# The first weights of a decoder-layer kernel in quarters, on two DMA queues

## The chip, the cores and the metric

The kernel runs on one core of one Trainium2 chip. The metric is the device time of one execution in microseconds. A time is given as the median of several runs; one execution was also taken by the hardware profiler, and all rows of the profile come from that one. TensorE (PE) multiplies matrices, VectorE (DVE) and ScalarE (ACT) work on tensors in SBUF, GpSimd (POOL) helps, and SyncE (SP) issues most DMAs. ScalarE can issue DMAs too, on a queue of its own (ACTq beside SPq).

## What is computed

One layer of a hybrid decoder on 256 tokens of width 2048, all in float32:

```python
h = rmsnorm(x, norm_mix_g)
u = h @ w_in                                  # ten column groups
ya = b_g * causal_dwconv3(c_g * xa, conv_w) * silu(za)
yb = rmsnorm_per_head(hgrn2_chunked(silu(q), kk, iv, log_f)) * hg_norm_g * silu(og)
m = sigmoid(ga) * (ya @ w_a_out) + sigmoid(gb) * (yb @ w_b_out)
x = x + m @ w_o
gate = sigmoid(rmsnorm(x, ple_norm_g) @ w_ple_gate)
x = x + gate * (p @ w_ple_proj)               # p: 256 tokens x 256 features
return rmsnorm(x, final_norm_g)
```

The part around the change is the first product of the program, `p @ w_ple_proj`: 256 features are two k tiles of 128, and the 2048 output columns are four groups of 512.

## The kernel before

A float32 operand is split into a high part in the float32r form and a low part, the rest (`cut` at L198 for weights: ScalarE copies the high part at L199, VectorE subtracts at L200; `put` at L318 for activations). A product is then three matmuls, high by high, high by low, low by high (L1157 to L1159). Activations are the stationary operand, 128 features by 128 tokens, and weights stream through, 512 columns at a time, into a PSUM bank for each of the two token tiles.

The whole program is one list, `items`, in an order written out by hand. An item is a chunk of two k tiles by 512 columns of one weight matrix, 512 KB. The first four items (`PP`) are w_ple_proj, one item for each group of 512 columns; item 4 (`FIRST`) begins the big projection w_in. The raw chunks of two items share a buffer (`raw`), are cut a few items ahead of their use into `whi` and `wlo`, and used by the loop at L1226.

At the start, eight matmuls on zeros keep TensorE busy (L1046). The first loads are issued by hand (L278 to L293): `load_half(pos, i, eng)` loads k tile i of item pos, 128 x 512 floats, 256 KB, on the queue of `eng`. ScalarE's queue carries the two halves of item 0; SyncE's carries p (`praw`, two k tiles of 128 x 256 floats, 128 KB each, L280), item 1, the parameters `prm_t` (36 KB, gains and small weights; L284), items 2 and 3, and then w_in and x. Each load takes the next of eight DMA counters in turn, so a load's issue waits for the landing of the load eight before it. ScalarE's own work in the same order stands behind its DMA issues: a table load (L303), then the cuts.

For items 0 to 2 the cuts go by halves, and for item 0 p's k tiles are put between them: `put_p(0)` (high part by VectorE, L323, low part at L326), first half of the weights, `put_p(1)` (high part by ScalarE, L325), second half. Item 0's matmuls have an order of their own, so that what is there first is used first:

```python
for a, b in ((0, hi), (1, hi), (0, lo)):
    for t in range(NT):
        nc.tensor.matmul(psum[t], state[opname][a][:, k, t * P : (t + 1) * P], b[:, s], ...)
```

Here `a` is the part of p (0 high, 1 low), `b` that of the weights, `t` the token tile, and `s` the 512 columns of k tile k. These are six matmuls for each k tile.

Of the kernel before, what the change touches and what calls it, by code (L numbers as in the profile page):

```python
# [15 lines left out]
P = 128  # L16
T = 256
NT = T // P
# [5 lines left out]
CW = 512  # L24
# [24 lines left out]
def hybrid_kernel(ctx, tc, xT, x, pT, prm, gfin, masks, w_in, w_a, w_b, w_o, w_pg, w_pp, out):  # L49
    nc = tc.nc  # L50
# [23 lines left out]
    state = {"tmp": "tmp1"}  # L74
# [3 lines left out]
    def nm(s):  # L78
        uid[0] += 1
        return f"{s}_{uid[0]}"  # L80
# [5 lines left out]
    def bank(tag):  # L86
        return ps.tile([P, CW], F32, tag=tag, bufs=4, name=nm(tag))
# [19 lines left out]
    items = []  # L107
# [21 lines left out]
    def raw_of(pos):  # L129
        it = items[pos]  # L130
        if it["raw"] not in loaded:
            if it["kind"] == "S" and it["op"] == "hT":
                t = tuple(
                    pools["st"].tile([P, n, CW], F32, tag=tag, bufs=bufs, name=nm(tag))
                    for tag, n, bufs in (("sA", 2, 2), ("sB", 1, 3))
                )
            else:
                n = it["c"] if it["j"] == 0 else 4 + 4 * (it["j"] - 1) + it["c"] // 2
                spare = it["op"] == "x1T" and n in (5, 10, 14)
                pool, bufs = (pools["late"], 1) if spare else (wp, 3)  # L140
                t = pool.tile([P, 2, 2 * CW], F32, tag="raw", bufs=bufs, name=nm("raw"))
            loaded[it["raw"]] = t
        return loaded[it["raw"]]

    def load(pos):
        it = items[pos]
        if it["raw"] not in loaded:
            raw, (w, g, c) = raw_of(pos), it["w"]
            if it["kind"] == "S" and it["op"] == "hT":
                for n, to in enumerate(raw):  # L150
                    nc.sync.dma_start(out=to.rearrange("p n x -> p (n x)"), in_=w[g + n, :, c, n * CW :])
            elif it["kind"] in ("S", "C"):
                for n in range(2):
                    nc.sync.dma_start(out=raw[:, n, :], in_=w[g + n, :, c, :])
            elif pos < APART:
                for i in range(2):
                    w, g, c = items[pos + i]["w"]
                    nc.sync.dma_start(out=raw[:, i, :], in_=w[g, :, c, :])
            else:
                nc.sync.dma_start(out=raw, in_=w[g, :, c : c + 2, :])  # L160
# [27 lines left out]
    def free_pair(until):  # L188
        if "back" not in state:
            held.append([until, pair_of(wp, 4)])  # L190
            del held[:-4]
            return held[-1][1]
        it = min(held, key=lambda it: it[0])
        assert it[0] < state["pos"]
        it[0] = until if until < last_group else len(items)
        return it[1]

    def cut(hi, lo, src):  # L198
        a = nc.scalar.activation(out=hi, in_=src, func=AF.Copy)  # L199
        v = nc.vector.tensor_tensor(out=lo, in0=src, in1=hi.bitcast(F32), op=ALU.subtract)  # L200
        state["splits"] = (a.ins, v.ins)

    def split(pos, halves=(0, 1)):
        it = items[pos]
        load(pos)
        src = raw_of(pos)
        if it["kind"] == "S" and it["op"] == "hT":
            src = src[0].rearrange("p n x -> p (n x)")
        else:
            src = src[:, it["slot"], :]  # L210
        if pos not in parts:
            parts[pos] = free_pair(pos)
        hi, lo = parts[pos]
        s = slice(halves[0] * CW, (halves[-1] + 1) * CW)
        cut(hi[:, s], lo[:, s], src[:, s])

    def combine_late(pos):
# [43 lines left out]
    prm_t = const.tile([P, PRM_N], F32, name="prm_t")  # L261
    praw = pools["tmp1"].tile([P, 1024], F32, tag="X", bufs=4, name="praw")[:, : 2 * T]
# [10 lines left out]
    def load_half(pos, i, eng):  # L273
        w, g, c = items[pos]["w"]
        s = slice(i * CW, (i + 1) * CW)
        eng.dma_start(out=raw_of(pos)[:, pos % 2, s], in_=w[g, :, c, s])

    load_half(0, 0, nc.scalar)  # L278
    for k in range(2):
        nc.sync.dma_start(out=praw[:, k * T : (k + 1) * T], in_=pT[:, k, :])  # L280
    load_half(0, 1, nc.scalar)
    for i in range(2):
        load_half(1, i, nc.sync)
    nc.sync.dma_start(out=prm_t, in_=prm)  # L284
    for c in (2, 3):
        for i in range(2):
            load_half(c, i, nc.sync)
# [473 lines left out]
    def ep_products(op, bk):  # L761
        for n in ("ga", "gb"):
            state[n] = t4(n, 1) if op == "hT" else t4()
        a0, a1, b0, b1 = quarters()
        nc.scalar.activation(out=a0, in_=bk["P1"], func=AF.Copy)
        add(b1, a0, bk["P6"])
        nc.vector.tensor_tensor(out=b0, in0=bk["P5"], in1=b1, op=ALU.subtract)
        add(a1, b1, bk["P7"])
        nc.vector.tensor_tensor(out=b1, in0=bk["P5"], in1=a1, op=ALU.subtract)

    def ep_gates(op, n, bk):
        q = quarters()
        for t in range(NT):
            add(q[2 * n + t], q[2 * n + t], bk["c", n, t])
        if op != "hT":
            active.append(ep_pg(n, q[2 * n : 2 * n + 2]))
            return
        for t in range(NT):
            d = q[2 * n + t]
            nc.scalar.activation(out=d, in_=d, func=AF.Sigmoid, scale=state["rstd1"][:, t : t + 1])  # L780
# [380 lines left out]
    def product(psum, op, k, t, hi, lo, first, last):  # L1161
        triple(psum, tuple(x[:, k, t * P : (t + 1) * P] for x in op), (hi, lo), first, last)
# [3 lines left out]
    def count_products(gi):  # L1166
        order = [it for it in items if it["kind"] in ("S", "C") and it["gi"] == gi]
        used.clear()
        left.clear()
        for it in order:  # L1170
            for name in names_of(it):
                left[name] = left.get(name, 0) + 1
# [53 lines left out]
    for pos, it in enumerate(items[:last_group]):  # L1226
        mark, state["pos"] = len(nc.cur_bb.bb.instructions), pos
        kind, j, c, last = (it[n] for n in ("kind", "j", "c", "last"))
        _, _, w, g, opname = groups[it["gi"]]
        nch = w.shape[2]  # L1230
# [48 lines left out]
        if pos == NORM + 4:  # L1279
# [3 lines left out]
            for i in range(4):  # L1283
                z = slice(i * Q, (i + 1) * Q)
                nc.sync.dma_start(out=near_m[z], in_=masks[z, :NARROW, z])
                nc.sync.dma_start(out=full_m[z, :, z], in_=masks[z, NARROW:, z])
        if kind in ("S", "C"):
            if c == 0 and it.get("n", 0) == 0:
                count_products(it["gi"])
                c00, c01, c10, c11 = (("c", i, t) for i in range(2) for t in range(NT))  # L1290
                order = ("P6", c01, "P5", "P7", "P1", c00, c10, c11)
                if it["op"] != "hT":
                    order = ("P1", "P6", "P5", "P7", c00, c01, c10, c11)
                for name, tag in zip(order, "ggggssss"):
                    banks[name] = bank(tag)
            if pos == settled + 2 or it["op"] == "hT" and kind == "C" and c == nch - 1 and it["n"] == 0:
                ep_products(it["op"], banks)
            unit_products(pos)
            if kind == "C" and c == nch - 1:
                ep_gates(it["op"], it["n"], banks)  # L1300
        else:
            if c == 0:
                psums[it["gi"]] = [bank("s" if kind == "PP" and j >= 2 else "g") for _ in range(NT)]
            psum = psums[it["gi"]]
            hi, lo = parts.pop(pos)
            for i in range(2):
                k = 2 * c + i
                s = slice(i * CW, (i + 1) * CW)
                if pos == 0:
                    for a, b in ((0, hi), (1, hi), (0, lo)):  # L1310
                        for t in range(NT):
                            nc.tensor.matmul(  # L1312
                                psum[t], state[opname][a][:, k, t * P : (t + 1) * P], b[:, s],
                                start=k == 0 and a == 0 and b is hi, stop=k == 2 * nch - 1 and b is lo,
                            )
                    continue
                for t in range(NT):
                    product(psum[t], state[opname], k, t, hi[:, s], lo[:, s], k == 0, k == 2 * nch - 1)
# [39 lines left out]
    for t, halves in ((0, (0, 1)), (1, (0,)), (1, (1,))):  # L1358
        bk, n = bank("g"), CW // 2
        for c in range(nlast):  # L1360
# [3 lines left out]
            hi, lo = parts[last_group + c]  # L1364
            for i in range(2):
                k = 2 * c + i
                s = slice(i * CW + halves[0] * n, i * CW + (halves[-1] + 1) * n)
# [86 lines left out]
```

## Time and profile before

| | |
|---|---|
| median of three runs | 813.72 us (812.8 to 813.87) |
| the profiled execution, its time | 812.97 us |
| its span in the profile | 811.2 us |
| PE busy | 801.2 us, 99% |
| DVE, ACT, POOL busy | 605.9, 462.9, 55.0 us |
| chain that ended last | PE 98%, issue 1%, DMA under 0.5% |

The span runs from the first to the last event in the profile; the time of the same execution is 1.8 us longer. Starts of instructions are counted from the start of the span. In a row of a timeline, the bracket at the end gives how long the engine sat idle ahead of the instruction, and what ended it. A time to landing runs from a DMA's issue to the moment at which a waiting engine can go on.

### The profile page before, as it was taken

The page shows a single profiled execution, that of the slowest core. Times are in us where ns is not written, and L with a number is a line of the kernel's source. Part 1 is how long each engine was busy: PE and PEld are TensorE (multiplying, and loading weights), DVE is VectorE, ACT ScalarE, POOL GpSimd, SP SyncE. Part 2 cuts the span into 40 slices and gives each one's busy share as a digit, 9 for nine tenths or more (in the row PEclk, how much of TensorE's full clock was granted, in tenths as well). Part 3 has the DMA queues.
Part 4 walks back from the last instruction along what each step waited for, and adds up shares of the span by engine and source line. Part 5 has one row for each costly group of instructions (what it writes and reads, how often), then busy time and mean ns, then how long its engine had stood idle before and what let it go on. Part 6 is the DMA issues. An engine that isn't in the chain of part 4 may idle for free.

```text
span 811.2 us, 10709 instructions
## 1 busy us (share of the span) xinstructions
PE 801.2 (99%) x4053; PEld 663.7 (82%) x4053; DVE 605.9 (75%) x785; ACT 462.9 (57%) x624; POOL 55.0 (7%) x59
## 2 busy tenths in 40 slices
PE   9999999999999999999999999999999999999995
PEld 6888888888888888888888888888888888888885
DVE  6846588767776498767679987987988666789953
ACT  7676476465555466466456556556554446665733
POOL 1000000001000000000021210110000000000160
PEclk9999999999999999999999999999999999999999
DMA  9988555648767555647799996995844778896702
GB/s 337 392 312 292 194 204 170 230 141 267 256 236 257 182 187 200 207 160 261 271 313 309 305 327 206 304 329 194 249 158 174 284 271 277 309 349 245 297 27 103
DMA packets 54099, 198.52 MB, mean 245 GB/s; under 512 B 6944, under 2 KB 16928, under 8 KB 40352
## 3 DMA queue, kind: packets, MB, share of 16 engines
q1 hardware_dynamic: 44640, 174.78, 60.5%
q0 software_dynamic: 6384, 16.25, 8.4%
q10 hardware_dynamic: 3024, 6.82, 2.4%
q8 instruction: 31, 0.51, 0.2%
q14 instruction: 20, 0.16, 0.1%
HBM read 184.19 MB, written 13.63 MB: 244 GB/s over the span
## 4 chain that ended last, share of the span: by engine, by line
PE 98%; issue 1%; DMA 0%; ACT 0%; DVE 0%; POOLq 0%; POOL 0%
PE g L1157 27%; PE g L1158 27%; PE g L1159 27%; PE s L1157 5%; PE s L1158 4%; PE s L1159 4%; PE s L539 1%; DMA raw<-in_w_pp 0%; PE g L1312 0%; PE s L640 0%; PE s L659 0%; PE s L658 0%; PE s L657 0%; PE s L631 0%; ACT xs L1006 0%
## 5 line engine op out<-in xcount | busy, mean ns | idle before, releaser
L200 DVE TENSOR_TENSOR wlo<-raw,whi 128x1024 fp32r<-128x1024 f32 (+1 forms) x255 | 304.0, 1209 | 141.1 <-ACT whi L199 139.1
L199 ACT ACTIVATE whi<-raw 128x1024 fp32r<-128x1024 f32 (+1 forms) x255 | 262.1, 1045 | 186.8 <-PE g L1159 158.1
L1157 PE MATMUL g<-whi,xh 128*128 128x512 f32 (+1 forms) x656 | 253.1, 386 | 0.0
L1159 PE MATMUL g<-whi,xl 128*128 128x512 f32 (+1 forms) x656 | 252.7, 385 | 0.0
L1158 PE MATMUL g<-wlo,xh 128*128 128x512 f32 (+1 forms) x656 | 252.7, 385 | 0.0
L1159 PEld LDWEIGHTS g<-whi,xl 128*128 128x128 f32 x656 | 123.2, 188 | 24.9
L1157 PEld LDWEIGHTS g<-whi,xh 128*128 128x128 f32 x656 | 123.2, 188 | 24.6
L1158 PEld LDWEIGHTS g<-wlo,xh 128*128 128x128 f32 x656 | 123.2, 188 | 24.2
L1158 PE MATMUL s<-wlo,xh 128*128 128x512 f32 x120 | 46.7, 389 | 0.0
L1157 PE MATMUL s<-whi,xh 128*128 128x512 f32 x120 | 46.5, 389 | 0.0
L1159 PE MATMUL s<-whi,xl 128*128 128x512 f32 x120 | 46.5, 389 | 0.0
L1158 PE MATMUL g<-wlo,mh 128*128 128x512 f32 x112 | 43.6, 389 | 0.0
L1159 PE MATMUL g<-whi,ml 128*128 128x512 f32 x112 | 43.5, 390 | 0.0
L1157 PE MATMUL g<-whi,mh 128*128 128x512 f32 x112 | 43.1, 389 | 0.0
L199 ACT ACTIVATE thi<-sA 128x1024 fp32r<-128x1024 f32 x15 | 15.9, 1062 | 32.8 <-DVE sA L756 20.3
L1159 PEld LDWEIGHTS s<-whi,xl 128*128 128x128 f32 x120 | 22.5, 188 | 4.7
L1157 PEld LDWEIGHTS s<-whi,xh 128*128 128x128 f32 x120 | 22.5, 188 | 4.7
L1158 PEld LDWEIGHTS s<-wlo,xh 128*128 128x128 f32 x120 | 22.5, 188 | 4.7
L1158 PE MATMUL g<-wlo,ybTh 128*128 128x512 f32 x64 | 24.9, 389 | 0.0
L1159 PE MATMUL g<-whi,ybTl 128*128 128x512 f32 x64 | 24.9, 389 | 0.0
L1157 PE MATMUL g<-whi,yaTh 128*128 128x512 f32 x64 | 24.9, 389 | 0.0
L1158 PE MATMUL g<-wlo,yaTh 128*128 128x512 f32 x64 | 24.9, 389 | 0.0
(272 smaller groups left out, 1075.8 us busy)
## 6 DMA issues: line engine op xcount, KB each, us to landing
raw<-in_w_in SPq DMA_DIRECT2D x66, 1024.0 KB, 4.8
raw<-in_w_o SPq DMA_DIRECT2D x16, 1024.0 KB, 6.3
sT<-in_w_in POOLq DMA_DIRECT2D x30, 512.0 KB, 9.5
raw<-in_w_in SPq DMA_DIRECT2D x28, 512.0 KB, 5.7
raw<-in_w_a SPq DMA_DIRECT2D x8, 1024.0 KB, 7.8
raw<-in_w_b SPq DMA_DIRECT2D x8, 1024.0 KB, 8.7
raw<-in_w_pg SPq DMA_DIRECT2D x16, 512.0 KB, 6.6
raw<-in_w_pg SPq DMA_DIRECT2D x8, 1024.0 KB, 6.7
```

The source lines that it names most:

```text
L199: a = nc.scalar.activation(out=hi, in_=src, func=AF.Copy)
L200: v = nc.vector.tensor_tensor(out=lo, in0=src, in1=hi.bitcast(F32), op=ALU.subtract)
L539: nc.tensor.matmul(out, X[:, 0, h, s], X[:, 1, h, t], start=True, stop=True, tile_position=(0, i * n))
L1157: nc.tensor.matmul(psum, oh, hi, start=first, stop=False)
L1158: nc.tensor.matmul(psum, oh, lo, start=False, stop=False)
L1159: nc.tensor.matmul(psum, ol, hi, start=False, stop=last)
```

## The change

Item 0's first half, k tile 0 of the weights, is loaded and cut in two quarters of 256 columns (128 KB each), the first on ScalarE's queue, the second on SyncE's. Item 0's matmuls for k tile 0 are 256 columns wide, with the first quarter's ahead of the second's in each of the three products; those for k tile 1 stay 512 wide. p's second k tile and the parameters go from SyncE's queue to ScalarE's.

```diff
@@ split
+        if pos == 0 and halves == (0,):
+            for u in range(2):
+                s = slice(u * CW // 2, (u + 1) * CW // 2)
+                cut(hi[:, s], lo[:, s], src[:, s])
+            return
         cut(hi[:, s], lo[:, s], src[:, s])
@@ first loads
-    load_half(0, 0, nc.scalar)
-    for k in range(2):
-        nc.sync.dma_start(out=praw[:, k * T : (k + 1) * T], in_=pT[:, k, :])
+    def load_p(k, eng):
+        eng.dma_start(out=praw[:, k * T : (k + 1) * T], in_=pT[:, k, :])
+
+    def load_quarter(i, eng):
+        s, (w, g, c) = slice(i * CW // 2, (i + 1) * CW // 2), items[0]["w"]
+        eng.dma_start(out=raw_of(0)[:, 0, s], in_=w[g, :, c, s])
+
+    load_quarter(0, nc.scalar)
+    load_p(0, nc.sync)
+    load_p(1, nc.scalar)
+    load_quarter(1, nc.sync)
     load_half(0, 1, nc.scalar)
+    nc.scalar.dma_start(out=prm_t, in_=prm)
     for i in range(2):
         load_half(1, i, nc.sync)
-    nc.sync.dma_start(out=prm_t, in_=prm)
@@ item 0's matmuls
                 if pos == 0:
+                    wide = CW // (2 - k)
                     for a, b in ((0, hi), (1, hi), (0, lo)):
-                        for t in range(NT):
-                            nc.tensor.matmul(
-                                psum[t], state[opname][a][:, k, t * P : (t + 1) * P], b[:, s],
-                                start=k == 0 and a == 0 and b is hi, stop=k == 2 * nch - 1 and b is lo,
-                            )
+                        for u in range(CW // wide):
+                            z = slice(u * wide, (u + 1) * wide)
+                            for t in range(NT):
+                                nc.tensor.matmul(
+                                    psum[t][:, z], state[opname][a][:, k, t * P : (t + 1) * P], b[:, s][:, z],
+                                    start=k == 0 and a == 0 and b is hi and u == 0, stop=k == 2 * nch - 1 and b is lo,
+                                )
```

SyncE at the start of the program, before. `praw` is p, `raw_85` the buffer of items 0 and 1 (`raw_93`, in the changed kernel `raw_94`, that of items 2 and 3), and DMAHW0 to 7 are the eight counters:

```order
1 L280 DMA praw<-in_pT 128x256 x2
2 L276 DMA raw_85<-in_w_pp 128x512 x2
3 L284 DMA prm_t<-in_prm 128x72
4 L276 DMA raw_93<-in_w_pp 128x512
5 L276 DMA raw_93<-in_w_pp 128x512 [waits DMAHW0_49]
6 L276 DMA raw_93<-in_w_pp 128x512 [waits DMAHW1_49]
```

SyncE at the same place in the changed kernel:

```order
1 L284 DMA praw<-in_pT 128x256
2 L288 DMA raw_85<-in_w_pp 128x256
3 L281 DMA raw_85<-in_w_pp 128x512 x2
4 L281 DMA raw_94<-in_w_pp 128x512 [waits DMAHW0_49]
5 L281 DMA raw_94<-in_w_pp 128x512 [waits DMAHW1_49]
6 L281 DMA raw_94<-in_w_pp 128x512 [waits DMAHW2_49]
```

p's second tile has given its place to the second quarter, the parameters are gone, and item 2's first half, which waited on nothing, now waits on the counter of the first quarter.

ScalarE at the start of the program, before; `whi_136` is item 0's high part, `pop` the cut p:

```order
1 L276 DMA raw_85<-in_w_pp 128x512 x2
2 L303 ACT_TABLE_LOAD
3 L303 ACTIVATE table_113<-mhalf 128x8 [waits Pool_49]
4 L199 ACTIVATE whi_136<-raw_85 128x512 [waits DMAHW0_49]
5 L325 ACTIVATE pop<-praw 128x256 [waits DMAHW2_49]
6 L199 ACTIVATE whi_136<-raw_85 128x512 [waits DMAHW3_49]
```

ScalarE in the changed kernel (`whi_137` is item 0's high part):

```order
1 L288 DMA raw_85<-in_w_pp 128x256
2 L284 DMA praw<-in_pT 128x256
3 L281 DMA raw_85<-in_w_pp 128x512
4 L295 DMA prm_t<-in_prm 128x72
5 L316 ACT_TABLE_LOAD
6 L316 ACTIVATE table_114<-mhalf 128x8 [waits Pool_49]
7 L199 ACTIVATE whi_137<-raw_85 128x256 [waits DMAHW0_49]
8 L199 ACTIVATE whi_137<-raw_85 128x256 [waits DMAHW3_49]
9 L338 ACTIVATE pop<-praw 128x256 [waits DMAHW2_49]
10 L199 ACTIVATE whi_137<-raw_85 128x512 [waits DMAHW4_49]
```

Four issues stand ahead of the table load instead of two, item 0's second half is third on the queue instead of second, and its cut stands behind three others instead of two.

TensorE's matmuls of item 0, k tile 0, before (`g_170` and `g_171` are the banks of the two token tiles):

```order
17 L1312 MATMUL g_170<-whi_136,pop 128x512 [waits DVE_49,Activation_49]
18 L1312 MATMUL g_171<-whi_136,pop 128x512
19 L1312 MATMUL g_170<-whi_136,pop 128x512 [waits DVE_49]
20 L1312 MATMUL g_171<-whi_136,pop 128x512
21 L1312 MATMUL g_170<-wlo_137,pop 128x512 [waits DVE_49]
```

TensorE at that place in the changed kernel:

```order
17 L1328 MATMUL g_173<-whi_137,pop 128x256 [waits DVE_49,Activation_49]
18 L1328 MATMUL g_174<-whi_137,pop 128x256
19 L1328 MATMUL g_173<-whi_137,pop 128x256 [waits Activation_49]
20 L1328 MATMUL g_174<-whi_137,pop 128x256
21 L1328 MATMUL g_173<-whi_137,pop 128x256 [waits DVE_49]
22 L1328 MATMUL g_174<-whi_137,pop 128x256
23 L1328 MATMUL g_173<-whi_137,pop 128x256
24 L1328 MATMUL g_174<-whi_137,pop 128x256
25 L1328 MATMUL g_173<-wlo_138,pop 128x256 [waits DVE_49]
```

The third matmul has a wait of its own on ScalarE, for the cut of the second quarter. Behind k tile 0 the order on every engine is as before.

## The prediction

> **What bounds the kernel now.** I read the page's totals first, then the chain of waits, TensorE's own waits, the first ten microseconds of each engine, and the DMA issues one at a time. The totals (busy us, share, instructions):
>
> ```profile
> span 811.2 us, 10709 instructions
> PE 801.2 (99%) x4053; PEld 663.7 (82%) x4053; DVE 605.9 (75%) x785; ACT 462.9 (57%) x624; POOL 55.0 (7%) x59
> ```
>
> TensorE is busy 99% of the span. The chain that ended last (start, us, what) and all of TensorE's waits in the whole program:
>
> ```profile
> 0.74 3.61 DMA raw<-in_w_pp
> 4.37 0.64 ACT whi L199
> 5.05 3.04 PE g L1312 x12
> ...
> PE s L1046 <- DVE warm L1042: 1.2, 1, 1.2
> PE g L1312 <- ACT whi L199: 0.3, 1, 0.3
> ```
>
> The chain is one load (landing at 4.35), one cut of it into a high part on ScalarE (L199), and then matmuls to the end. After 5.05 us TensorE waits for nothing. So an edit of the first 8 us is worth exactly the shift of the moment from which TensorE runs without a gap, and the time cannot gain more than a part of those 5.05 us. The start, engine by engine (start, us, engine, line, operation):
>
> ```profile
> 1.19 3.59 PE L1046 MATMUL s<-warm 128*128 128x512 bf16 x8 [1.19 <-DVE warm L1042]
> 0.74 0.89 ACTq L276 DMA_DIRECT2D raw<-in_w_pp  x2
> 1.66 1.28 ACT L303 ACT_TABLE_LOAD   x1 [1.66 <-PEq L1443]
> 2.96 0.21 ACT L303 ACTIVATE table<-mhalf 128x8 f32<-128x8 f32 x1
> 4.37 0.63 ACT L199 ACTIVATE whi<-raw 128x512 fp32r<-128x512 f32 x1 [1.21 <-DMA raw<-in_w_pp]
> 4.96 0.42 ACT L325 ACTIVATE pop<-praw 128x256 fp32r<-128x256 f32 x1
> 5.36 0.63 ACT L199 ACTIVATE whi<-raw 128x512 fp32r<-128x512 f32 x1
> 6.42 2.08 ACT L199 ACTIVATE whi<-raw 128x512 fp32r<-128x512 f32 x3 [0.42 <-DMA raw<-in_w_pp]
> 4.18 0.29 DVE L323 CAST pop<-praw 128x256 fp32r<-128x256 f32 x1 [3.04 <-DMA praw<-in_pT]
> 4.50 0.43 DVE L326 TENSOR_TENSOR pop<-praw,pop 128x256 fp32r<-128x256 f32 x1
> 5.04 0.69 DVE L200 TENSOR_TENSOR wlo<-raw,whi 128x512 fp32r<-128x512 f32 x1
> ```
>
> The loads of the start, one issue each, in windows around 0.9, 1.2 and 1.7 us (queue, KB, us from issue to landing):
>
> ```profile
> raw<-in_w_pp ACTq DMA_DIRECT2D x1, 256.0 KB, 3.6
> praw<-in_pT SPq DMA_DIRECT2D x1, 128.0 KB, 3.4
> ...
> raw<-in_w_pp ACTq DMA_DIRECT2D x1, 256.0 KB, 4.2
> praw<-in_pT SPq DMA_DIRECT2D x1, 128.0 KB, 3.8
> ...
> raw<-in_w_pp SPq DMA_DIRECT2D x1, 256.0 KB, 4.7
> ```
>
> The reader should see two things. A load of half the size lands only 0.2 us sooner (3.4 against 3.6), and each further place in a queue costs more: first, second, third on SyncE's queue are 3.4, 3.8 and 4.7. Matmul rates come from four stretches (length, then PE busy and count; a stretch that ends on a start counts it):
>
> ```profile
> 5.05:6.55 1.50, 1.50 (x7) 1.24 (x7) 1.50 (x3) 1.08 (x3) 0.00 (x0) 1.00 1.01 370
> 6.55:7.93 1.38, 1.38 (x7) 1.13 (x6) 1.02 (x3) 1.20 (x3) 0.00 (x0) 1.00 1.00 375
> 7.93:10.65 2.72, 2.72 (x13) 2.25 (x12) 1.92 (x3) 1.28 (x3) 0.00 (x0) 1.00 1.05 395
> 790.95:795.26 4.31, 4.31 (x37) 4.31 (x36) 2.23 (x8) 2.36 (x7) 0.56 (x1) 1.00 0.00 0
> ```
>
> Matmuls 512 wide follow each other every 2.72 / 12 = 0.227 us; those 256 wide, near the end of the program, every 4.31 / 36 = 0.120 us.
>
> **The change part by part.** Call the 512 columns of weights for p's k tile 0 "W0", now two quarters W0a and W0b, and those for k tile 1 "W1".
>
> *Matmuls.* Six of 512 columns become twelve of 256: 12 x 0.120 - 6 x 0.227 = 1.44 - 1.36 = +0.08 us on TensorE, on the path.
>
> *First quarter.* W0a is first on ScalarE's queue with 128 KB. Between 3.4 and 3.6 us from the issue at 0.74 it lands at 4.14 to 4.34; I take 3.4, the row of that size. ScalarE must be free: two more issues at 0.45 us each (0.89 us for two) move its table load and the small activation from 3.17 to 4.06, so it is, by 0.08 us. The cut takes 0.42 us as L325 does for 256 columns, and TensorE followed 0.05 us behind the cut (4.37 + 0.63 to 5.05). First matmul at 4.61 instead of 5.05. In that alone there is 0.44 us.
>
> *Second quarter.* W0b takes the place that p's second tile had, second on SyncE's queue, issued at about 1.19: 3.8 us, seen at 4.99 (3.4 would make it 4.59; the load beside it is smaller now). Cut to 5.41, TensorE at 5.46. Only two of the twelve matmuls lie ahead of it, the hi-by-hi ones of W0a (to 4.85), so TensorE stands from 4.85 to 5.46, and the other ten end at 5.46 + 10 x 0.120 = 6.66. Before, k tile 0 ended at 6.55. The early start is already used up: +0.11. VectorE cuts 2 x 0.43 instead of 0.69, its second low part done near 5.9, used at 6.4: hidden.
>
> *Second k tile.* This is the term that decides. W1 was second on ScalarE's queue and is now third, issued at 0.74 + 2 x 0.45 = 1.64 instead of 1.19. Second there took 4.2 us (5.84 for the new issue), third on SyncE's queue 4.7 (6.34). The bytes ahead of it in its own queue are the same 256 KB as before, which speaks for 4.2; it shares the engines with SyncE's third load more closely than before, which speaks for 4.7. Neither row is nearer, so I take the middle, 4.45: seen at 6.09, against 5.36. The two cuts ahead of it on ScalarE (W0b and p's tile, 0.4 us each from 4.99) are done by 5.8 and don't delay it. With 0.63 + 0.05 TensorE begins k tile 1 at 6.77. Before it began at 6.55. Ends: with 4.2, 6.52, which lies under the 6.66 of k tile 0, so +0.11; with 4.7, 7.02, +0.47.
>
> A stretch before shows the engines' rate (GB/s last, DMA share ahead of it):
>
> ```profile
> 1.90:4.20 2.30, 2.30 (x7) 0.76 (x5) 0.02 (x1) 1.25 (x2) 0.73 (x2) 1.00 0.90 305
> 4.20:5.20 1.00, 0.73 (x3) 0.15 (x2) 0.86 (x3) 0.83 (x2) 0.00 (x0) 1.00 0.61 200
> 5.20:8.00 2.80, 2.80 (x13) 2.28 (x14) 2.44 (x5) 2.20 (x5) 0.00 (x0) 1.00 1.02 377
> ```
>
> From 4.2 to 5.2 the engines were only 61% busy, so W1 can use room that was free; that is why I don't take 4.7. The Trainium skill, "DMA: Bandwidth & Descriptors", section "Issuing engines are not separate DMA queues", says that loads issued by different engines run on the same 16 DMA engines and interleave. By that rule alone W1 and SyncE's third load, queued side by side, land together at the 6.36 of the latter, and the sum would be near +0.47 instead of +0.22.
>
> *SyncE's queue.* Its fourth row in the order shown with the change has got a wait. The load of the third chunk's first half, issued at 3.07 without a wait, now waits for W0a (counter DMAHW0, 4.14), so it goes out 1.1 us later; behind it stand the other weights and x. Two 256 KB loads are still queued ahead of it, 512 KB, 1.4 us at 377 GB/s, so the engines keep busy, and it costs nothing; rival C is the price if they don't. The parameters leave SyncE's queue (one issue of 0.43 us) and are last of four on ScalarE's; their first reader is L328:
>
> ```profile
> 10.57 1.06 ACT L199 ACTIVATE whi<-raw 128x1024 fp32r<-128x1024 f32 x1 [0.79 <-DMA raw<-in_w_pp]
> 12.54 0.91 ACT L328 ACTIVATE xh<-t,prm_t 128x256 fp32r<-128x256 f32 x2 [0.42 <-DMA t<-in_xT]
> 11.67 1.22 DVE L200 TENSOR_TENSOR wlo<-raw,whi 128x1024 fp32r<-128x1024 f32 x1 [1.16 <-ACT whi L199]
> ```
>
> Issued near 2.1, the parameters have ten microseconds: nothing. Behind W1 on ScalarE stands the next chunk's first half, cut from about 6.7 to 7.3; TensorE wants it at 6.77 + 1.38 = 8.15: hidden, and so is its low part on VectorE (8.15, wanted at 8.38), by 0.2 us only.
>
> *Sum.* +0.22 us: 6.77 - 6.55. The profiled execution took 812.97 us (span 811.2), so 813.2; the median of the runs shown, 813.72, lies 0.75 above it, and moved by the same it is 813.9.
>
> **The rivals.** *A: a small gain.* W0b lands as soon as a first load (3.4 us, seen at 4.59) and W1 at the old 5.36. Then TensorE starts W0b at 5.06, k tile 0 ends at 6.26, W1's cut (third in line on ScalarE, from 5.4) is ready at 6.1: 6.26 - 6.55 = -0.29 us, 813.4. For it: the free room at 4.2 to 5.2. Against it: W1 would have to land 3.7 us after its issue, and the one load in third place took 4.7.
>
> *B: the clock, and slower by more than can be missed.* The eight warm-up matmuls take 3.59 us, 0.45 each, half the rate of one every 0.227 us; the first real one shows the change of rate (ns, least, median, most):
>
> ```profile
> L1312 PE MATMUL g<-whi,pop x8: 389/396/497, 5.1 to 7.2; 128*128 128x512 f32 x8
> ```
>
> One took 497 ns, half of them 396 or less. So TensorE needed from 1.19 to about 5.06, 3.9 us with a gap of 0.3, to get the full rate. If the new gap (0.6 us after two matmuls, then 0.1 before W1) makes it miss that, another such stretch runs at half the rate: 3.9 / 2 = +1.9 us, 815.6. It decides if the full rate has not come by 4.85. Against it: the gap begins where it did before, and is only 0.4 us longer. The Trainium skill, "TensorE: Matmul & The Clock Gate", Part 1, has the clock released after a busy window of about 3.4 us that runs freely, whenever the kernel starts; by its figure a missed window costs an estimated 1.7 us. No row here shows where a window begins.
>
> *C: the later loads.* If all weights from the third chunk on and x come 1.1 us later, the fourth chunk's low part (11.67 + 1.22 = 12.89) comes at 13.99, wanted at 7.93 + 2 x 2.72 + 0.23 = 13.60, now 13.82: another 0.17, and x behind it about as much: +0.5, 814.2. It decides when the loads are over 0.9 us late.
>
> **How the numbers follow.** Forecast 0.60, A 0.22, C 0.10, B 0.08. The three runs shown span 812.8 to 813.87, so 0.2% (1.6 us) is about what a measurement of this kernel can tell from no change. Only B passes it: slower 0.08; faster by that much has no mechanism, 0.02 for chance between chips; within, 0.90. Range: A from the lowest run, 812.8 - 0.3 = 812.5, to the late end of the forecast, +0.47, and C from the highest, 814.4; a little past it, 814.6, for W1 still later.
>
> **What would show it.** Right: the first matmul near 4.6, a wait for ScalarE's cut of W0b near 4.9 to 5.5, a second wait for W1 ending near 6.8, and no wait after. A is right if k tile 1 starts before 6.5; B if 512-wide matmuls beyond 6 us stand 0.45 apart; C if TensorE waits again between 13 and 17 us. Wrong altogether: a change of more than a microsecond with these starts unmoved, or TensorE already full at 4.2.

## The result and the profile after

| | before | changed |
|---|---|---|
| median, first comparison (21 runs each) | 813.02 us (812.74 to 815.47) | 814.33 us (813.76 to 817.44) |
| median beside the experiments | 813.23 us (30 runs) | 815.39 us (814.94 to 817.67, 10 runs) |
| profiled execution, its time and span | 812.97, 811.2 us | 817.44, 814.8 us |

The changed kernel is slower: the ratio is 1.0019 (95% interval 1.0013 to 1.0025) in the first comparison and 1.0031 (1.0021 to 1.0040) when it was run once more, as `after_same`, beside other kernels. That is 1.3 and 2.2 us in the medians, where the forecast had 0.2. The execution profiled first is the slowest of its 21 runs, so it is read together with the second one.

TensorE at the start of the changed kernel (start, us, line, tiles, shape, count; in the bracket the idle time ahead and what ended it):

```profile
4.49 0.79 PE L1328 MATMUL g<-whi,pop 128*128 128x256 f32 x2
5.85 1.65 PE L1328 MATMUL g<-whi,pop 128*128 128x256 f32 x6 [0.56 <-ACT whi L199]
7.30 1.05 PE L1328 MATMUL g<-wlo,pop 128*128 128x256 f32 x4
8.15 1.91 PE L1328 MATMUL g<-whi,pop 128*128 128x512 f32 x4
9.86 0.99 PE L1328 MATMUL g<-wlo,pop 128*128 128x512 f32 x2
10.68 0.40 PE L1170 MATMUL g<-whi,pop 128*128 128x512 f32 x1
```

The first matmul is at 4.49 instead of 5.05 (forecast 4.61). But item 1 (L1170) begins at 10.68, where it began at 7.93 before: 2.75 us later. Two things lie between. TensorE stands after the two matmuls of W0a, and from 5.85 it runs at half its rate: the four hi-by-hi and lo-by-hi matmuls from 8.15 to 9.86 are 1.71 / 4 = 0.43 us apart, against 0.227 before. At 10.68 the full rate has come. ScalarE in the same execution:

```profile
3.92 0.21 ACT L316 ACTIVATE table<-mhalf 128x8 f32<-128x8 f32 x1
4.04 0.40 ACT L199 ACTIVATE whi<-raw 128x256 fp32r<-128x256 f32 x1
5.38 0.42 ACT L199 ACTIVATE whi<-raw 128x256 fp32r<-128x256 f32 x1 [0.94 <-DMA raw<-in_w_pp]
5.70 0.40 ACT L338 ACTIVATE pop<-praw 128x256 fp32r<-128x256 f32 x1
6.80 2.79 ACT L199 ACTIVATE whi<-raw 128x512 fp32r<-128x512 f32 x5 [0.70 <-DMA raw<-in_w_pp]
```

W1's cut starts at 6.80 (forecast 6.09, before 5.36). At the full rate TensorE would have begun k tile 1 at 6.80 + 0.63 + 0.05 = 7.48 and item 1 at 7.48 + 1.38 = 8.86. So W1 alone would have cost 0.93 of the 2.75 us, and the rate brought the other 1.82. As it ran, though, TensorE came to k tile 1 only at 8.15, when W1's high part had been done since 7.43 and no row shows a wait for it: in this execution the wait for the second quarter and the half rate made the loss, and W1 was hidden behind them. In the middle of the program this execution had one more wait of 0.6 us, which the second one did not have (all of TensorE's waits, us in total, times, longest):

```profile
PE s L1059 <- DVE warm L1055: 1.2, 1, 1.2
PE s L1171 <- DVE blo L200: 0.6, 1, 0.6
PE g L1328 <- ACT whi L199: 0.6, 1, 0.6
```

2.75 + 0.6 is 3.4 of the 3.6 us by which the span grew; the rest isn't traced. The second execution, `after_same` (span 813.8 us), reached the same 10.68 by another way:

```profile
5.64 0.98 PE L1328 MATMUL g<-whi,pop 128*128 128x256 f32 x6 [0.54 <-ACT whi L199]
6.46 0.64 PE L1328 MATMUL g<-wlo,pop 128*128 128x256 f32 x4
9.18 1.20 PE L1328 MATMUL g<-whi,pop 128*128 128x512 f32 x4 [2.09 <-ACT whi L199]
10.22 0.62 PE L1328 MATMUL g<-wlo,pop 128*128 128x512 f32 x2
10.68 0.40 PE L1170 MATMUL g<-whi,pop 128*128 128x512 f32 x1
```

Here the rate was full from 5.64 on (six matmuls 256 wide in 0.82 us to 6.46), and W1 alone set the start of k tile 1: 2.09 of the 2.75 us are TensorE's wait for it. ScalarE got it at 8.50:

```profile
8.50 2.71 ACT L199 ACTIVATE whi<-raw 128x512 fp32r<-128x512 f32 x5 [2.60 <-DMA raw<-in_w_pp]
```

### The profile page after: what moved, and what is told of

Read it like the earlier page. It is cut to its first block, busy times and chain, and to the rows that moved or that the text cites. A ratio compares the mean times of both kernels' runs of the same rounds, so it can differ in the third digit from the quotient of the medians.

```text
span 814.8 us, 10725 instructions
## 1 busy us (share of the span) xinstructions
PE 804.0 (99%) x4059; PEld 666.1 (82%) x4059; DVE 605.7 (74%) x786; ACT 463.0 (57%) x625; POOL 55.0 (7%) x59
## 4 chain that ended last, share of the span: by engine, by line
PE 95%; DMA 2%; DVE 1%; issue 1%; ACT 1%; POOLq 0%; POOL 0%; SPq 0%
PE g L1170 27%; PE g L1172 27%; PE g L1171 27%; PE s L1171 4%; PE s L1172 4%; PE s L1170 4%; DMA sA<-in_w_in 1%; PE g L1328 1%; PE s L552 1%; DMA raw<-in_w_pp 1%; DVE tlo L200 0%; PE s L653 0%; PE s L671 0%; PE s L672 0%; PE s L670 0%
## 5 line engine op out<-in xcount | busy, mean ns | idle before, releaser
L200 DVE TENSOR_TENSOR wlo<-raw,whi 128x1024 fp32r<-128x1024 f32 (+2 forms) x256 | 304.0, 1205 | 146.4 <-ACT whi L199 144.9
L199 ACT ACTIVATE whi<-raw 128x1024 fp32r<-128x1024 f32 (+2 forms) x256 | 262.1, 1042 | 191.8 <-PE g L1172 161.0
L1170 PE MATMUL g<-whi,xh 128*128 128x512 f32 (+1 forms) x656 | 253.1, 386 | 0.0
L1170 PEld LDWEIGHTS g<-whi,xh 128*128 128x128 f32 x656 | 123.2, 188 | 24.7
L1170 PE MATMUL s<-whi,xh 128*128 128x512 f32 x120 | 46.5, 389 | 0.0
L1170 PE MATMUL g<-whi,mh 128*128 128x512 f32 x112 | 43.1, 389 | 0.0
L1170 PEld LDWEIGHTS s<-whi,xh 128*128 128x128 f32 x120 | 22.5, 188 | 4.6
L1170 PE MATMUL g<-whi,yaTh 128*128 128x512 f32 x64 | 24.9, 389 | 0.0
```

Source lines behind the costliest of these rows:

```text
L1170: nc.tensor.matmul(psum, oh, hi, start=first, stop=False)
```

## The experiments

Three questions: does the loss come from the matmuls or the loads; if the loads, from W1's place in its queue or from the quarters; and what does the gap ahead of the products do to TensorE's rate. The kernels of each set shared their runs of the kernel before (median 813.23 in the first two sets, 812.96 in the last). Ratios are to it.

**The cuts and matmuls alone.** `cut_only` is the kernel before with these lines of the change:

```diff
+        if pos == 0 and halves == (0,):
+            for u in range(2):
+                s = slice(u * CW // 2, (u + 1) * CW // 2)
+                cut(hi[:, s], lo[:, s], src[:, s])
+            return
...
+                    wide = CW // (2 - k)
```

> The kernel before with the cuts and matmuls of the change alone: item 0's first half is loaded whole, as before, but cut and used in two quarters of 256 columns. Theory 1 (the moved loads set the loss, through the late second quarter and the late second k tile): first matmul at 4.37 + 0.42 + 0.05 = 4.84 us instead of 5.05, k tile 1 at about 6.45, no loss; 813.0 us, within 0.3 us of the kernel before. Rival (the twelve narrow matmuls and the extra cuts cost by themselves): slower by 0.3 us or more, towards 814.

Measured 813.04 us, ratio 0.9999 (0.9990 to 1.0008). Its first matmul came at 4.85, and TensorE waited for nothing after that. The rival falls: quarter cuts and narrow matmuls cost nothing that shows, and don't gain either.

**The loads alone.** `loads_only` is the changed kernel without those lines.

> The changed kernel's loads, queues and order, but item 0's first half cut whole and used by matmuls of 512 columns as before. Theory 1 (loads): both quarters must have landed, near 5.2 us, so the first matmul comes at about 6.0 and k tile 1 waits for the second half as in the changed kernel, near 7.5: about as slow as the changed kernel, 814.3 us (+1.0 to +1.5). Rival (narrow matmuls and cuts): back near the kernel before, 813.0 to 813.3.

Measured 815.36 us in 6 runs, ratio 1.0031 (1.0019 to 1.0043), as slow as the changed kernel beside it. The first matmul came at 5.35 and not at 6.0, since both quarters had landed by 4.67; but W1 reached ScalarE at 7.39:

```profile
4.67 0.63 ACT L199 ACTIVATE whi<-raw 128x512 fp32r<-128x512 f32 x1 [0.54 <-DMA raw<-in_w_pp]
5.21 0.40 ACT L333 ACTIVATE pop<-praw 128x256 fp32r<-128x256 f32 x1
7.39 2.19 ACT L199 ACTIVATE whi<-raw 128x512 fp32r<-128x512 f32 x4 [1.78 <-DMA raw<-in_w_pp]
```

TensorE in the same execution:

```profile
5.35 2.07 PE L1320 MATMUL g<-whi,pop 128*128 128x512 f32 x4 [0.57 <-ACT whi L199]
7.22 1.05 PE L1320 MATMUL g<-wlo,pop 128*128 128x512 f32 x2
8.08 1.81 PE L1320 MATMUL g<-whi,pop 128*128 128x512 f32 x4
9.72 0.62 PE L1320 MATMUL g<-wlo,pop 128*128 128x512 f32 x2
```

So the loss is in the loads. W1 set the start of k tile 1 at 8.08 (7.39 + 0.63 + 0.05 = 8.07), 1.53 us later than before. But this execution ran at half the rate too: item 1 began at 10.18, 2.10 us after k tile 1 instead of 1.38, so 0.7 us of its loss are the rate.

**One load ahead of W1.** `p1_ahead` moves only p's second k tile:

```diff
-    for k in range(2):
-        nc.sync.dma_start(out=praw[:, k * T : (k + 1) * T], in_=pT[:, k, :])
+    for k, eng in ((0, nc.sync), (1, nc.scalar)):
+        eng.dma_start(out=praw[:, k * T : (k + 1) * T], in_=pT[:, k, :])
```

> The kernel before with one load moved: p's second k tile goes from SyncE's queue to ScalarE's, ahead of the weights' second k tile W1, which is so third there, as in the changed kernel; no quarters, parameters on SyncE's queue. Theory 1a (the third place on ScalarE's queue makes W1 late): W1 lands 5 us or more after its issue, k tile 1 waits for it until 7.3 or later, +0.7 to +1.2 us, 814.0 to 814.4. Rival 1b (the quarter loads in 1 KB rows on both queues make everything behind them late): W1 lands near 5.4 to 5.9, within 0.3 us of the kernel before.

Measured 814.46 us, ratio 1.0019 (1.0010 to 1.0028). With no quarters in it, W1 landed 5.0 us after its issue, against 4.2 before (queue, KB, us to landing), and TensorE waited 0.9 us for it:

```profile
raw<-in_w_pp ACTq DMA_DIRECT2D x1, 256.0 KB, 5.0
...
4.82 1.19 PE L1312 MATMUL g<-whi,pop 128*128 128x512 f32 x4 [0.43 <-ACT whi L199]
5.85 0.63 PE L1312 MATMUL g<-wlo,pop 128*128 128x512 f32 x2
7.38 0.97 PE L1312 MATMUL g<-whi,pop 128*128 128x512 f32 x3 [0.90 <-ACT whi L199]
```

k tile 1 began at 7.38 instead of 6.55, at the full rate. This one edit is enough for a loss as in the first comparison. It also lets SyncE's two loads of item 1 go out 0.47 us sooner, and they landed at 5.2 and about 6.4, ahead of W1 at 6.7; before, W1 landed at 5.4 and the first of them at 6.4. The engines were no slower: from 4.2 to 5.2 they moved 366 GB/s, against 200 before.

**Quarters, with the old bytes ahead.** `quarters_one_queue` has the changed kernel's cuts, matmuls and quarter loads, but this order:

```diff
     load_quarter(0, nc.scalar)
     load_p(0, nc.sync)
-    load_p(1, nc.scalar)
-    load_quarter(1, nc.sync)
+    load_quarter(1, nc.scalar)
+    load_p(1, nc.sync)
     load_half(0, 1, nc.scalar)
-    nc.scalar.dma_start(out=prm_t, in_=prm)
     for i in range(2):
         load_half(1, i, nc.sync)
+    nc.sync.dma_start(out=prm_t, in_=prm)
```

> The changed kernel with both quarters on ScalarE's queue, ahead of W1, and p and the parameters on SyncE's queue as before; cuts and matmuls as changed. W1 is third on ScalarE's queue here too, behind the same 256 KB as before the change. Theory 1a (third place): W1 late, k tile 1 at 7.3 or later, +0.7 or more. Theory 1b (quarter loads): late as well, both quarters' 1 KB rows being there. Rival 1c (bytes ahead decide): W1 at 5.4 to 5.9 as in the kernel before, within 0.3 us of it, and the second quarter near 4.6.

Measured 815.07 us, ratio 1.0025 (1.0015 to 1.0034). W1, third behind two quarters, landed 5.6 us after its issue, k tile 1 began at 7.98 after a wait of 1.2 us. Rival 1c falls: the bytes ahead in its own queue are the same 256 KB as before, and W1 is late all the same.

**W1 second again.** `w1_second` is the changed kernel with p's second tile third on SyncE's queue:

```diff
-    load_p(1, nc.scalar)
-    load_quarter(1, nc.sync)
+    load_quarter(1, nc.sync)
+    load_p(1, nc.sync)
```

> The changed kernel with p's second k tile back on SyncE's queue, third there behind the second quarter; W1 is second on ScalarE's queue. Theory 1a (third place): W1 lands near 5.4 as before the change, p's second tile is now the late one at about 6, and k tile 1 starts near 6.9 instead of 7.5: 0.4 to 0.6 us faster than the changed kernel, 813.7. Rival 1b (quarter loads make everything late): as slow as the changed kernel, 814.3.

Measured 813.51 us, ratio 1.0004 (0.9995 to 1.0013), against 815.39 for the changed kernel beside it. W1 landed 3.7 us after its issue and p's second tile in 3.7 too, so k tile 1 began at 6.36, sooner than the 6.55 of before. Nearly the whole loss of the change goes with this one move, quarters, narrow matmuls and the parameters' place all kept. Rival 1b falls as the main cause. That the tile in third place on SyncE's queue came early, at 5.37, was not expected. It shows that a third place alone doesn't make a load late: the parameters, third on ScalarE's queue here, landed 3.9 us after their issue, and SyncE's first 256 KB of item 1, now fourth, in 4.2.

**The changed kernel again.**

> The changed kernel once more, unchanged, beside these three and as a second trace of it. Expected: W1 lands 5 to 6 us after its issue and k tile 1 waits for it; 814.3 us. If its lateness is chance of the one execution, W1 lands under 4.7 us after its issue in this trace.

Measured 815.39 us; its trace is shown above. W1 took 6.8 us to land, later than expected, so its lateness is no chance of the first trace, but its size varies: 5.1 and 6.8 us in two executions.

**W0 in two loads with long rows.** `w0_by_rows` splits W0 by partitions in the kernel before:

```diff
-    load_half(0, 0, nc.scalar)
+    w0, g0, c0 = items[0]["w"]
+    for i in range(2):
+        z = slice(i * P // 2, (i + 1) * P // 2)
+        nc.scalar.dma_start(out=raw_of(0)[z, 0, :CW], in_=w0[g0, z, c0, :CW])
```

> The kernel before with the first 256 KB of weights (W0) loaded by two DMAs of 64 partitions each, both on ScalarE's queue, so that W1 is third there, behind as many bytes as before and behind 128 rows of 2 KB as before (two quarters of 256 columns would be 256 rows of 1 KB); cuts and matmuls as before. Theory 1r (the rows queued ahead decide): W1 lands 4.0 to 4.4 us after its issue, as second before, k tile 1 at most 0.3 us later, 813.2 to 813.6. Theory 1a (the third place decides, whatever stands ahead): 5 us or more, k tile 1 at 7.3 or later, 814.0 or more.

Measured 815.99 us in 5 runs (814.71 to 817.12), ratio 1.0036 (1.0023 to 1.0049). W1 landed 5.2 us after an issue at 1.97 (1.66 in the other kernels with W1 third), and W0 itself was whole only at 5.54, against 4.37:

```profile
5.54 0.63 ACT L199 ACTIVATE whi<-raw 128x512 fp32r<-128x512 f32 x1 [1.43 <-DMA raw<-in_w_pp]
6.08 0.40 ACT L328 ACTIVATE pop<-praw 128x256 fp32r<-128x256 f32 x1
7.16 2.72 ACT L199 ACTIVATE whi<-raw 128x512 fp32r<-128x512 f32 x5 [0.68 <-DMA raw<-in_w_pp]
```

Theory 1r falls. The price of a load more, ahead on the same queue, is there with rows of 2 KB too.

**The gap alone.** `gap_only` is the kernel before with `WARM = 6` in place of 8.

> The kernel before with six warm-up matmuls instead of eight, so that TensorE stands idle from about 3.75 to 5.05 us; loads and everything else as before. Theory 2 (an idle stretch of about a microsecond ahead of the first products puts off the moment at which TensorE gets its full rate): the first product still starts at 5.05, but 512-wide matmuls 0.43 us apart go on up to several us longer in some executions; median +0.5 to +1.5 us, the slowest runs +2 to +3.5. Rival (the clock comes at a fixed time after the first matmul whatever the gap): within 0.2 us of the kernel before.

Measured 814.75 us (814.22 to 815.09), ratio 1.0017 (1.0008 to 1.0025); each of its 11 runs lies above each of the 28 of the kernel before beside it (812.62 to 814.08). No load moved, yet the start reads:

```profile
4.94 2.07 PE L1312 MATMUL g<-whi,pop 128*128 128x512 f32 x4 [1.00 <-ACT whi L199]
6.81 1.05 PE L1312 MATMUL g<-wlo,pop 128*128 128x512 f32 x2
7.66 1.88 PE L1312 MATMUL g<-whi,pop 128*128 128x512 f32 x4
9.37 0.63 PE L1312 MATMUL g<-wlo,pop 128*128 128x512 f32 x2
9.84 0.39 PE L1157 MATMUL g<-whi,pop 128*128 128x512 f32 x1
```

The first product even starts 0.1 us sooner, and item 1 begins at 9.84 instead of 7.93: the first twelve matmuls take 4.90 us instead of 2.88. So two warm-up matmuls fewer cost 1.5 us in the median by the rate alone. The spread I expected did not come; all runs were late alike. And the gap's length is not what counts by itself: `w0_by_rows` stood idle even longer ahead of its first product, after eight warm-up matmuls (from TensorE's waits, us in total, times, longest),

```profile
PE g L1315 <- ACT whi L199: 1.4, 1, 1.4
```

and its item 1 began at 9.32, 1.48 us after k tile 1 at 7.84: the full rate. Nor do eight warm-up matmuls ensure it: the first execution of the changed kernel and `loads_only` had eight, and missed it.

The traces' record of the granted clock tells more: it has the moment at which the full rate came. Before, that was 5.05. The stretch at the full rate from there to beyond the last matmul lasts 798.7, 802.1 or 805.5 us in every one of the 13 traces, though it starts anywhere from 3.85 to 10.64; these lengths are 3.41 us apart. So the rate changes only at moments 3.41 us apart, and where these lie differs from execution to execution. As an estimate of how much work a stretch of 3.41 us needs, I count 0.43 us for each 512-wide and 0.21 for each 256-wide matmul at half rate:

| execution | full rate from | busy us of the 3.41 ahead of it | of the 3.41 before those |
|---|---|---|---|
| before | 5.05 | 2.94 | 0.44 |
| p1_ahead | 3.85 | 2.66 | none |
| w0_by_rows | 5.21 | 2.78 | 0.60 |
| changed, after_same | 4.75 | 3.37 | 0.14 |
| changed, first | 10.64 | 3.41 | 2.31, and 2.62 before |
| loads_only | 9.44 | 3.25 | 2.48 |
| gap_only | 9.38 | 3.41 | 2.04 |

In all 13 traces about 2.66 us or more were enough and about 2.62 or less were not. Counted so, six warm-up matmuls are 2.6 us together and eight are 3.4. By this estimate six can't be enough by themselves, and eight are, if the stretch holds most of them. What a gap does depends on the stretch in which it falls: in `after_same` the full rate had come before the gap, and in `w0_by_rows` it came in the middle of it.

**The gap filled in the changed kernel.** `after_filled` has `WARM = 10`.

> The changed kernel with ten warm-up matmuls instead of eight, so that TensorE stays busy to about 5.46 us. The first product comes later by 1 us, but the second quarter and the second half bind anyway. Theory 1 + 2 (loads set the least time, the clock the spread above it): least time as in the changed kernel, 813.8, but without its slow runs: median 813.9, none above 814.8. Rival (loads alone, no part of the clock): the same spread as the changed kernel, median 814.3, some runs at 816 to 817. Rival (a later first product costs): slower by up to 0.9.

Measured 815.19 us (813.82 to 815.82), ratio 1.0021 (1.0012 to 1.0029), against 815.39 (814.94 to 817.67) for the changed kernel in the next set. The median I expected was wrong: W1 landed 6.5 us after its issue and bound alone. In the trace the full rate was there from 6.05 on, and of the 11 runs none lies above 815.82. That fits a share of the clock in the slowest runs only; it doesn't prove it, since the two were not in one set.

**A ninth warm-up matmul.** `warm9` has `WARM = 9` in the kernel before, and `cut_fill` in `cut_only`.

> The kernel before with nine warm-up matmuls, which end at 5.03 us where the first product starts at 5.05: the gap of 0.3 us is filled and nothing else changes. If the short gap costs anything: 0.2 to 0.5 us faster, 812.8. If only a long gap does: within 0.15 us of the kernel before.

> The cuts and matmuls of the change with the loads of before, and nine warm-up matmuls instead of eight, which end at 5.03 us where the first product would come at 4.86: TensorE has no gap left. If a gap of 0.1 to 0.4 us already puts off the full rate in some executions: 0.2 to 0.5 us faster than the kernel before, 812.8. If only a long gap does: 813.0 to 813.2, no difference.

Measured 813.08 us, ratio 1.0001 (0.9992 to 1.0010), and 813.24 us, 1.0006 (0.9997 to 1.0015). The gap of 0.3 us before costs nothing that can be seen. No version beat the kernel before.

W1's way over all profiled executions, with its place on ScalarE's queue:

| kernel | W1's place | us from issue to landing | start of k tile 1 | start of item 1 | median, us |
|---|---|---|---|---|---|
| before | 2 | 4.2 | 6.55 | 7.93 | 813.0 to 813.2 |
| cut_only | 2 | 4.2 | 6.45 | 7.84 | 813.04 |
| w1_second | 2 | 3.7 | 6.36 | 7.85 | 813.51 |
| p1_ahead | 3 | 5.0 | 7.38 | 8.88 | 814.46 |
| quarters_one_queue | 3 | 5.6 | 7.98 | 9.47 | 815.07 |
| w0_by_rows | 3 | 5.2 | 7.84 | 9.32 | 815.99 |
| loads_only | 3 | 5.7 | 8.08 | 10.18 | 815.36 |
| after_filled | 3 | 6.5 | 8.87 | 10.36 | 815.19 |
| changed, two executions | 3 | 5.1, 6.8 | 8.15, 9.18 | 10.68, 10.68 | 814.33, 815.39 |

In every kernel with W1 second it lands within 4.2 us, and in every kernel with W1 third it takes 5.0 or more. The traces show what lies between: from 1.50 to W1's landing the DMA engines moved 0.96 MB before (3.86 us at 248 GB/s) and 0.87 in `w1_second`, but 1.59 in `p1_ahead` (5.18 us at 307 GB/s), 1.49 in `quarters_one_queue`, 1.56 in `w0_by_rows`, and 1.58 and 1.82 in the changed kernel. So W1 was late mainly because half a megabyte or more of other loads was moved ahead of it.

## Why the prediction was right, and where it was not

*What bounds the kernel.* Right: the shift of the moment from which TensorE runs without a gap is the shift of the end. `after_same` began item 1 2.75 us later, and its span is 2.6 us longer; `p1_ahead` 0.95 and 0.9.

*First quarter.* Right: forecast 4.61, measured 4.49 in both executions. The quarter landed even sooner (3.1 us), and ScalarE's table load, moved back by two issues, held the cut until 4.04, within 0.02 us of the forecast.

*Second quarter.* Right in kind: TensorE stood after two matmuls, and the early start was used up. It landed 4.2 and 4.0 us after its issue instead of 3.8, so its first matmul came at 5.85 and 5.64, not at 5.46.

*Second k tile.* This is the step that was mis-sized, and the one I had said would decide. I took 4.45 us, the middle of 4.2 and 4.7, on the ground that engines only 61% busy from 4.2 to 5.2 had room for W1. Measured 5.1 and 6.8. In the second execution this alone set the start of k tile 1, at 9.18 instead of the 6.77 of the forecast; in the first the half rate hid it. The same stretches after (GB/s last, DMA share ahead of it), in the changed kernel's first execution:

```profile
1.90:4.20 2.30, 2.30 (x7) 0.76 (x5) 0.44 (x2) 1.56 (x3) 0.73 (x2) 1.00 0.96 270
4.20:5.20 1.00, 1.00 (x4) 0.50 (x2) 0.70 (x2) 0.24 (x1) 0.00 (x0) 1.00 0.92 326
```

and in its second:

```profile
1.90:4.20 2.30, 2.30 (x7) 0.73 (x5) 0.36 (x2) 1.56 (x3) 0.73 (x2) 1.00 0.79 220
4.20:5.20 1.00, 0.90 (x4) 0.40 (x2) 0.70 (x2) 0.27 (x2) 0.00 (x0) 1.00 0.95 273
```

The room was used (92% and 95%), but the first 2.3 us moved less than before, 270 and 220 GB/s against 305. Idle engines were no sign of a transfer that would land sooner. The interleaving rule of the Trainium skill ("DMA: Bandwidth & Descriptors", "Issuing engines are not separate DMA queues"), whose sum I put at +0.47, lay nearer than my value. By it W1 should have come with SyncE's third load; that took 4.6 and 5.9 us from its issue, W1 5.1 and 6.8, so W1 came later still.

*SyncE's queue and the parameters.* Right: neither trace shows a wait of TensorE between item 1 and 20 us. Rival C did not happen.

*Rival A.* Fell: W1 would have had to land 3.7 us after its issue. In second place it did, in `w1_second`.

*Rival B.* Given 0.08, and it happened in one of two profiled executions, at about its price: 1.82 us against 1.9. `gap_only` shows the mechanism alone. I had tied it to the gap's length, and that was wrong: the gap read 0.56 us in the execution that missed the full rate and 0.54 in the one that had it, and `w0_by_rows` had it after 1.4. What counts is how busy the stretch of 3.41 us is in which the gap falls. The Trainium skill ("TensorE: Matmul & The Clock Gate", Part 1) has the clock released by a busy window of about 3.4 us that runs freely. The traces agree, with steps of 3.41 us that begin at another moment in each execution; a window needn't be busy throughout, since 2.66 us of it were enough in `p1_ahead`. The twelve matmuls of `gap_only` took 2.0 us longer; a missed window by the page's figure is an estimated 1.7. That six warm-up matmuls made all its 11 runs late fits this, but only one of them was traced; nor is it known how many runs of the changed kernel missed the full rate.

*The numbers.* 814.33 lies in the range of 812.5 to 814.6, with the sign forecast, 1.3 us above before instead of 0.2, and at the edge of the 0.2% that I called no change. The second median, 815.39, lies outside the range, and its ratio of 1.0031 is past the 0.2%, which had been given 0.08. The upper end of the range came from rival C, which did not happen, and from a W1 landing 4.7 us after its issue, which was too early. So that the first median lies inside is in part luck; the likeliest value was too low.

What stays open: why so much goes ahead of W1 when one more load stands before it, and why that varies between executions. A load more ahead was shown to matter, with rows of 1 KB and of 2 KB. But it also puts W1's issue off, from 1.19 to 1.66 or 1.97, so that SyncE's 256 KB loads go out with it or ahead of it; the later issue and the place in the queue were not separated. `p1_ahead` (5.0), without any split of W0, lies below all others in third place, so splitting W0 may add to it; that was not separated.

## What to carry to other kernels

When the program's start waits on loads, find the last of the first loads that the bound engine needs, and keep it early in its queue: getting the first matmul half a microsecond sooner was worth nothing, while one small load put ahead of that last one cost over a microsecond. Price a moved load by all that is issued on either queue before it or with it, not by the bytes ahead in its own queue or by idle DMA engines. And when warm-up matmuls are there for the clock, keep enough of them: the rate can cost more than the load they wait for.

## What was not expected of the hardware

- W1's 256 KB took 5.0 to 6.8 us from issue to landing as third load on ScalarE's queue, 3.7 to 4.2 as second. But the parameters (36 KB) in third place there took 3.9, and 128 KB in third place on SyncE's queue 3.7 (both `w1_second`).
- Two loads of 64 partitions (128 KB each) gave W0 at 5.54 us, one of 128 partitions (256 KB) at 4.37.
- Six warm-up matmuls instead of eight kept TensorE at half its rate to about 9.4 us in the one trace that has it (1.5 us in the median, all 11 runs slower), while an idle stretch of 1.4 us after eight left it at the full rate in one trace, and nine were no better than eight. After eight, two of nine profiled executions missed it as well.
- The full rate came only at moments 3.41 us apart, which lie differently in each execution, and by an estimate only after 3.41 us of which TensorE was busy for 2.66 or more (13 traces).
